# Which engine makes the low halves and the sums on SBUF tiles: chosen by stage

## The chip, the cores and the metric

One core of one Trainium2 chip runs the kernel. The metric is the device time of one execution in microseconds (us), the median of a few runs. Besides, one execution was recorded by the hardware profiler. Its rows use these names: PE is TensorE (matmuls), PEld its weight loads, DVE VectorE, ACT ScalarE, POOL GpSimd, SP SyncE, which issues nearly all DMAs here.

## The reference

One decoder layer in float32 with 2048 tokens, a width of 1024 and a hidden width of 2816:

```python
h = rmsnorm(x, g_mix[i])
z = h @ w_in[i]
zb, zc, zx, zq, zk, zv = jnp.split(z, ..., axis=-1)
y_c = zb * causal_dwconv3(zc * zx, conv_w[i], conv_b[i])
y_a = dilated_attention(rmsnorm(q), rmsnorm(k), v)
y = jnp.concatenate([rmsnorm(y_c, g_out_conv[i]), rmsnorm(y_a, g_out_attn[i])], axis=-1)
x = x + y @ w_out[i]                                        # the projection
h = rmsnorm(x, g_ffn[i])
gate = causal_dwconv3(h @ w_gate[i], ffn_conv_w[i], ffn_conv_b[i])
x = x + (jax.nn.silu(gate) * (h @ w_up[i])) @ w_down[i]     # gate and up, then the down-projection
ple_gate = jax.nn.sigmoid(rmsnorm(x, g_ple[i]) @ w_ple_gate[i])
x = x + ple_gate * (p[i].astype(x.dtype) @ w_ple_proj[i])
```

## The kernel before

Every float32 product is made of three fast matmuls. An operand x is split into a high half (`hi`, a cast by ACT, line 93) and a low half (`lo = x - hi`, a subtraction of two SBUF tiles, line 94), and `mm3` (line 97) adds hi·hi, hi·lo and lo·hi in PSUM. So each weight tile costs PE its matmuls, ACT one cast, and DVE or POOL one subtraction of 128x512 elements.

The program has three parts. `qkv` makes queries, keys and values. `mix` runs the attention and, in the gaps of it, the first convolution branch (`conv`): the product `zps`, the three taps (`ext`, `tap`, lines 248 to 257), the result `yc` (line 327), which also frees one of two PSUM banks. `rest`, which the change touches, is a list of stages that run one after the other:

- `project`, three times: y @ w_out in PSUM tiles of 128 tokens x 512. `split_y` (lines 824, 825) makes the operands `t` and `g` from y; `square` (lines 828, 830) sums the squares of y into `u`; `reciprocal_root` and `rsqrt` (lines 75 to 84, 838, 840: `ssy`, `rs_h` to `rsy`) make the factor by which line 902 scales a finished bank, adds x and so frees the bank.
- `prepare`, between them: `right` builds the seven right-hand operands of a Strassen-like product (seven instead of eight block products) from four blocks: four sums t1 to t4 (line 722), seven splits (`put`).
- `gate_up` for each half of the tokens: 11 blocks of hidden columns, each with seven products for the gate and seven for up. `left` makes the seven left operands (sums on line 702, splits on 94). In the first half `sums_of_w_down` also forms four differences of blocks of w_down (line 959, tile `g`) and stores them in DRAM (`td`), and `for_later` normalizes the other half's tokens.
- `down` for each half: seven products over 11 blocks, whose weights `raw` come from `td` or w_down; `finished` adds the parts (lines 1048, 1051).
- `ple`: the last two products.

Weights come from `stream`: it loads the next `raw` ahead of its use and has three split operands `w` made ahead of the one in use. The order of each engine's queue is not written by hand: a scheduler with a model of its own places the instructions, and each engine then works through its queue in that order, waiting on semaphores. `shared()` (line 87) gives DVE or POOL in turn for work that both can do: the splits of `stream` and `left`, the sums of `square`, the first sum in `finished`.

Of the kernel before, what the change touches and what calls it, by code (L numbers as in the profile page):

```python
# [16 lines left out]
ALU = mybir.AluOpType  # L17
# [22 lines left out]
class Layer:  # L40


    def __init__(self, tc, a, out, ctx):
        self.tc, self.nc, self.a, self.out, self.ctx = tc, tc.nc, a, out, ctx
        nc = self.nc
        self.turn = 0
        self.const = ctx.enter_context(tc.tile_pool(reuse_waits="tile", name="const", bufs=1))
        self.dram = ctx.enter_context(tc.tile_pool(name="dram", bufs=1, space=DRAM))
        self.ident = self.const.tile([P, P], F32, name="ident")
        make_identity(nc, self.ident)  # L50
        d = self.dram
        self.hd = [d.tile([KD, P, QT], F32, name=f"hd{c}") for c in range(NQ)]
        self.qd = [d.tile([2, 2, HD, SEQ], F32, name=f"qd{p}") for p in range(4)]
        self.kd = [d.tile([2, 2, HD, SEQ], F32, name=f"kd{p}") for p in range(4)]
        self.vd = [d.tile([QT, NH, 2 * HD], F32, name=f"vd{c}") for c in range(NQ)]
        self.ycd = [d.tile([P, SEQ], F32, name=f"ycd{i}") for i in range(4)]
        self.yad = [d.tile([P, SEQ], F32, name=f"yad{i}") for i in range(4)]
        self.xd = [[[d.tile([P, D], F32, name=f"xd{i}{c}{j}") for j in range(4)] for c in range(NQ)] for i in range(3)]
        self.gd = [d.tile([7, NF // 2, P, QT], F32, name=f"gd{h}") for h in range(2)]
        self.bd = [[d.tile([P, D], F32, name=f"bd{i}{j}") for j in range(4)] for i in range(2)]  # L60
        self.td = [d.tile([NF // 2, P, 2, 512], F32, name=f"td{i}") for i in range(2)]
        self.xq, self.pq, self.oq = [t.rearrange("(c j r) m -> c j r m", c=NQ, r=P) for t in (a["x"], a["p"], out)]
# [23 lines left out]

    def shared(self):

        self.turn = (self.turn + 1) % 3
        return self.nc.vector if self.turn else self.nc.gpsimd  # L90

    def split(self, hi, lo, src, lo_engine):
# [558 lines left out]
    def rest(self):  # L651
        nc, tc, a = self.nc, self.tc, self.a
        stages = [("project", (0, 1), (0,)), ("project", (0, 1), (1,)), ("prepare", 0), ("project", (2, 3), (0, 1)),
                  ("gate_up", 0), ("prepare", 1), ("down", 0), ("gate_up", 1), ("prepare_ple",), ("down", 1), ("ple",)]
        with ExitStack() as st:
# [59 lines left out]
            def right(at, b11, b12, b21, b22, temps, lo_engine):  # L715

                def put(i, x, engine):
                    hi, lo = at(i)
                    self.split(hi, lo, x, engine)

                t1, t2, t3, t4 = temps
                minus = lambda t, x, y: nc.vector.tensor_tensor(t, x, y, ALU.subtract)
                put(0, b11, lo_engine)
                yield
                minus(t1, b12, b11)
                put(4, t1, nc.vector)
                yield
                minus(t3, b22, b12)
                put(2, b22, lo_engine)
                yield  # L730
                minus(t2, b22, t1)
                put(6, t3, nc.vector)
                yield
                put(1, b21, lo_engine)
                yield
                minus(t4, b21, t2)
                put(5, t2, nc.gpsimd)
                yield
                put(3, t4, nc.gpsimd)
                yield  # L740

            def products(ops, quad, done):
# [169 lines left out]
            def prepare(h):  # L912
                self.quad = [new_quad(i > 3) for i in range(7)]
                if h:
                    for j in range(4):
                        b = [row("u") for _ in range(4)]
                        for x, (i, g) in zip(b, ((0, 0), (1, 0), (0, 1), (1, 1))):
                            nc.sync.dma_start(x, self.bd[i][j][:, 512 * g:512 * g + 512])
                        b = [x.rearrange("p (k n) -> p k n", n=P) for x in b]
                        yield from right(halves(self.quad, slice(j * P, j * P + P)), *b, [b[0], b[3], b[1], b[2]], nc.vector)  # L920
                    return
                self.g_ffn = gain("g_ffn")
                r = roots(0, 0, 8)
                for j in range(4):
                    xs = [load_tile(self.xd[1][i][j]) for i in range(2)]
                    for i, x in enumerate(xs):
                        normalize(x, r[:, 4 * i + j:4 * i + j + 1], self.g_ffn)
                    yield
                    b1 = []
                    for x in xs:  # L930
                        t = row("u").rearrange("p (k n) -> p k n", n=P)
                        nc.scalar.copy(t, transposed(x, 0))
                        b1.append(t)
                    b22, b21 = transposed(xs[1], 1), transposed(xs[0], 1)
                    for _ in right(halves(self.quad, slice(j * P, j * P + P)), *b1, b21, b22,
                                   [x[:, i:i + 512].rearrange("p (k n) -> p k n", n=P) for x in xs for i in (0, 512)], nc.vector):
                        pass
                    yield
# [14 lines left out]
            def sums_of_w_down(f):  # L953

                b = [operand("g").bitcast(F32) for _ in range(2)]
                for i, t in enumerate(b):
                    n = (2 * f + i) * P
                    nc.sync.dma_start(t.rearrange("p s n -> p (s n)"), a["w_down"][n:n + P])
                minus = lambda t, x, y: nc.vector.tensor_tensor(t, x, y, ALU.subtract)
                (b11, b12), (b21, b22) = [[t[:, s] for s in range(2)] for t in b]  # L960
                minus(b11, b12, b11)
                minus(b12, b22, b12)
                minus(b22, b22, b11)
                minus(b21, b21, b22)
                for d, t in zip(self.td, b):
                    nc.sync.dma_start(d[f], t)

            def gate_up(h):
                if h == 0:
                    background[0] = for_later()  # L970
                for f in range(NF // 2):
# [40 lines left out]
                    if h == 0:  # L1012
                        sums_of_w_down(f)
# [58 lines left out]
            def prepare_ple():  # L1072
                self.g_ple = gain("g_ple")
                self.quad = [new_quad(i > 3) for i in range(7)]
                for k in range(4):
                    b = [row("u") for _ in range(4)]
                    for x, (i, n) in zip(b, ((0, 0), (0, 1), (1, 0), (1, 1))):
                        nc.sync.dma_start(x, a["w_ple_gate"][(k + 4 * i) * P:(k + 4 * i + 1) * P, 512 * n:512 * n + 512])
                    yield from right(lambda i: (self.quad[i][:, k, 0], self.quad[i][:, k, 1]), *b,
                                     [b[0], b[3], b[1], b[2]], nc.vector)  # L1080
# [71 lines left out]
            ws = self.stream(raw_pool, operand, left, 3, stages)  # L1152
            run = dict(project=project, prepare=prepare, gate_up=gate_up, down=down, prepare_ple=prepare_ple, ple=ple)
            for name, *arg in stages:
                if name not in ("project", "down"):
                    for _ in background[0]:
                        pass
                if name.startswith("prepare"):
                    background[0] = run[name](*arg)
                    continue  # L1160
                run[name](*arg)
# [57 lines left out]
```

## Time and profile before

| what | value |
|---|---|
| median of 3 runs | 2756.98 us (2752.61 to 2761.0) |
| the profiled execution | 2758.95 us |
| its span from the first to the last instruction | 2757.2 us |
| PE busy | 2621.5 us, 95% of the span |
| DVE busy | 2006.8 us, 73% |
| ACT busy | 1321.2 us, 48% |
| POOL busy | 784.3 us, 28% |
| mean granted TensorE clock | 0.983 |

The profiled execution is 2.0 us above the median, and 1.75 us of it lie outside its span. The granted clock is the share of full speed (2.4 GHz) that TensorE was given; a fall shows as its lower level, half of that.

### The profile page before, as it was taken

Reading aid. Unit: us, or ns where it says so; the run is one execution under the profiler, and the core shown is the slowest. Engines: PE = TensorE matmul, PEld = TensorE weight load, DVE = VectorE, ACT = ScalarE, POOL = GpSimd, SP = SyncE. Lnnn points to the kernel's source line nnn. Section 1 sums busy time; section 2 is a strip of 40 time slices with the busy share of each in tenths; the row PEclk is TensorE's granted clock in tenths of the full one; section 3 lists DMA queues with packets and bytes.
Section 4 is the critical chain, followed back from the end, with each engine's and each line's share of the span. In section 5 each row is a group of like instructions: output and inputs, shape, how many; then the busy total and the mean of one; then the engine's idle time right before and its main releaser. Section 6 shows DMA issues by size and latency. Waiting matters only on the chain. (4 is left out here: it accounts for less than half of the span.)

```text
span 2757.2 us, 37506 instructions
## 1 busy us (share of the span) xinstructions
PE 2621.5 (95%) x12320; PEld 2169.0 (79%) x12320; DVE 2006.8 (73%) x3878; ACT 1321.2 (48%) x2941; POOL 784.3 (28%) x527
## 2 busy tenths in 40 slices
PE   7999989999999989899999999989999999998999
PEld 5777878888888778777788888767888887877887
DVE  8766656867677665998888778567888877557655
ACT  3332357877777344454344345444444435444332
POOL 5111311524343621123222223122222223223332
PEclk9999989999999999999999999999999999999999
DMA  5544565665756688568633346663323336666332
GB/s 191 153 138 123 169 163 139 184 184 146 205 154 180 220 279 296 196 228 274 241 114 105 107 142 227 216 233 115 102 101 107 104 111 218 220 217 204 103 130 85
DMA packets 283860, 470.04 MB, mean 170 GB/s; under 512 B 32656, under 2 KB 101904, under 8 KB 283664
## 3 DMA queue, kind: packets, MB, share of 16 engines
q1 hardware_dynamic: 283664, 467.64, 53.4%
q8 instruction: 97, 1.59, 0.2%
q14 instruction: 99, 0.81, 0.1%
HBM read 339.53 MB, written 127.99 MB: 170 GB/s over the span
## 5 line engine op out<-in xcount | busy, mean ns | idle before, releaser
L97 PE MATMUL ps<-t,w 128*128 128x512 f32 x4368 | 1024.3, 395 | 16.1 <-DVE w L94 9.5
L97 PEld LDWEIGHTS ps<-t,w 128*128 128x128 f32 x4368 | 819.6, 188 | 207.7 <-DVE w L94 12.4
L97 PE MATMUL ps<-w,g 128*128 128x512 f32 x1368 | 339.0, 397 | 26.9 <-DVE t L902 6.2
L97 PEld LDWEIGHTS ps<-w,g 128*128 128x128 f32 x1368 | 257.3, 190 | 89.0 <-DVE t L902 7.3
L94 POOL TENSOR_TENSOR w<-raw,w 128x512 fp32r<-128x512 f32 x100 | 144.9, 1449 | 564.1 <-ACT w L93 364.0
L97 PE MATMUL zps<-hq,chi 128*128 128x512 f32 x768 | 256.8, 411 | 5.3 <-DVE yc L327 5.3
L93 ACT CAST w<-raw 128x512 fp32r<-128x512 f32 x318 | 193.7, 616 | 119.5 <-PE ps L97 111.7
L289 POOL TENSOR_TENSOR clo<-craw,chi 128x512 fp32r<-128x512 f32 x96 | 126.4, 1322 | 389.8 <-ACT chi L288 144.2
L93 ACT CAST w<-s 128x512 fp32r<-128x512 f32 x208 | 128.3, 619 | 224.7 <-PE ps L97 200.5
L97 PE MATMUL ps<-w,t 128*128 128x512 f32 x852 | 211.6, 394 | 9.1 <-DVE w L94 5.9
L94 POOL TENSOR_TENSOR w<-s,w 128x512 fp32r<-128x512 f32 x70 | 111.8, 1597 | 368.7 <-ACT w L93 300.0
L438 ACT ACTIVATE pt<-so,md 128x256 f32<-128x256 f32 (+1 forms) x384 | 175.1, 458 | 79.9 <-DVE md L435 78.0
L97 PEld LDWEIGHTS ps<-w,t 128*128 128x128 f32 x852 | 159.0, 188 | 49.5 <-DVE w L94 8.8
L94 DVE TENSOR_TENSOR w<-raw,w 128x512 fp32r<-128x512 f32 x218 | 177.1, 816 | 15.5 <-ACT w L93 15.5
L435 DVE CUSTOM_DVE_ANT_0 so<-s,neg 128x256 f32<-128x256 f32 (+1 forms) x384 | 130.4, 362 | 60.9 <-PE s L432 47.3
L97 PEld LDWEIGHTS zps<-hq,chi 128*128 128x128 f32 x768 | 142.3, 195 | 29.6 <-DVE yc L327 6.1
L97 PE MATMUL zps<-hq,clo 128*128 128x512 f32 x384 | 154.3, 402 | 0.0
L432 PE MATMUL s<-kk,qs 128*128 128x256 f32 (+1 forms) x384 | 136.8, 360 | 11.8 <-DMA kk<-kd 9.1
L431 PE MATMUL s<-kk,qs 128*128 128x256 f32 (+1 forms) x384 | 132.8, 352 | 14.7 <-DMA kk<-kd 12.2
L471 DVE TENSOR_TENSOR nb<-po,nb 64x512 f32<-64x512 f32 x96 | 92.2, 961 | 65.0 <-ACT nb L470 64.2
L94 DVE TENSOR_TENSOR g<-g 128x512 fp32r<-128x512 f32 x84 | 72.6, 867 | 88.5 <-ACT g L93 88.5
L453 DVE TENSOR_TENSOR plo<-ptp,phi 128x512 fp32r<-128x512 f32 (+1 forms) x160 | 103.6, 653 | 30.9 <-ACT phi L452 30.2
(221 smaller groups left out, 4917.4 us busy)
## 6 DMA issues: line engine op xcount, KB each, us to landing
gd<-t SPq DMA_DIRECT2D x110, 256.0 KB, 2.0
craw<-in_w_conv_dram SPq DMA_DIRECT2D x96, 256.0 KB, 4.0
raw<-in_w_gate_dram SPq DMA_DIRECT2D x44, 512.0 KB, 3.8
raw<-in_w_up_dram SPq DMA_DIRECT2D x44, 512.0 KB, 3.7
g<-gd SPq DMA_DIRECT2D x84, 256.0 KB, 5.1
raw<-td SPq DMA_DIRECT2D x40, 512.0 KB, 4.5
t<-gd SPq DMA_DIRECT2D x70, 256.0 KB, 4.6
v<-vd SPq DMA_DIRECT2D x264, 64.0 KB, 2.7
```

Of the source, the lines that this page charges most:

```text
L93: self.nc.scalar.copy(hi, src)
L94: lo_engine.tensor_tensor(lo, src, hi.bitcast(F32), ALU.subtract)
L97: mm = lambda *a, **k: self.nc.tensor.matmul(*a, **k, **kw)
L289: nc.gpsimd.tensor_tensor(lo, raw, hi.bitcast(F32), ALU.subtract)
L431: mm(s[:, lo:], qb[l], cols[0], start=True, stop=False)
L432: mm(s[:, lo:], qb[l], cols[1], start=False, stop=True)
L435: nc.vector.tensor_tensor_reduce(out=so[:, lo:], in0=s[:, lo:], in1=neg[:, br, lo:], scale=-slope, scalar=3.0e38, op0=ALU.add, op1=ALU.min ...
L438: nc.scalar.activation(pt[:, l, lo:], so[:, lo:], AF.Exp, bias=md[:, 0, col:col + 1], scale=-1.0, accum_out=md[:, 1, col:col + 1])
L453: nc.vector.tensor_tensor(lo[:, i:i + n], tp[:, :n], hi[:, i:i + n].bitcast(F32), ALU.subtract)
L471: nc.vector.tensor_tensor(dst, like(po[other], br), dst, ALU.add)
```

## The change

Turns are counted in a cycle that the stage sets: 1 in `project`, so that every `shared()` is POOL; 2 in `down`; 3 elsewhere, as it was everywhere. In `right` the splits of t1 to t4 no longer have an engine of their own (two DVE, two POOL) but take turns, too. In `sums_of_w_down` two of the four differences go to POOL. The stage also decides for the generators that run in its background, as `prepare` does within `project` and `down`.

```diff
     def shared(self):
 
-        self.turn = (self.turn + 1) % 3
+        self.turn = (self.turn + 1) % self.cycle
         return self.nc.vector if self.turn else self.nc.gpsimd
...
                 minus(t1, b12, b11)
-                put(4, t1, nc.vector)
+                put(4, t1, self.shared())
...
-                put(6, t3, nc.vector)
+                put(6, t3, self.shared())
...
-                put(5, t2, nc.gpsimd)
+                put(5, t2, self.shared())
                 yield
-                put(3, t4, nc.gpsimd)
+                put(3, t4, self.shared())
...
-                minus = lambda t, x, y: nc.vector.tensor_tensor(t, x, y, ALU.subtract)
+                minus = lambda t, x, y: (nc.vector if t is b21 or t is b22 else nc.gpsimd).tensor_tensor(t, x, y, ALU.subtract)
...
             for name, *arg in stages:
+                self.cycle = dict(project=1, down=2).get(name, 3)
```

In the built programs 99 instructions of 128x512 elements change from DVE to POOL. Up to the end of the projection they are 23 splits of `w`, 16 sums of squares and 8 splits in `right` (which has 16 on POOL there, and had 8); of the 22 differences of w_down that move (22 stay), 7 stand in POOL's queue ahead of the first sums of `gate_up` on line 1007 and 15 behind; each `down` has 12 or 13 more splits on POOL. The sums of `finished` stay at 12 and 12. The scheduler places the rest of the queues anew. In the rows below the lines after the change are one higher than before (two from line 1156 on).

DVE's queue at the end of the convolution branch, from the reciprocal of the attention's denominators (`mx`) to the result `yc`. Before:

```order
L515 RECIPROCAL mx<-mx 32x128
L94 TENSOR_TENSOR w<-raw,w 128x512
L516 TENSOR_TENSOR e<-e,mx 32x384
L256 SCALAR_TENSOR_TENSOR tap<-ext,cw,tap 128x512
L94 TENSOR_TENSOR w<-raw,w 128x512
L257 SCALAR_TENSOR_TENSOR tap<-ext,cw,tap 128x512
L94 TENSOR_TENSOR w<-raw,w 128x512
L288 CAST chi<-craw 128x512
L94 TENSOR_TENSOR w<-raw,w 128x512
L327 TENSOR_TENSOR yc<-zps,tap 128x512
```

The same place after the change:

```order
L516 RECIPROCAL mx<-mx 32x128
L322 TENSOR_TENSOR ext<-zps,zc 128x512
L253 COPY ext<-carry 128x2
L517 TENSOR_TENSOR e<-e,mx 32x384
L249 COPY ext<-ext 128x2x31
L255 COPY carry<-ext 128x2
L257 SCALAR_TENSOR_TENSOR tap<-ext,cw,tap 128x512
L258 SCALAR_TENSOR_TENSOR tap<-ext,cw,tap 128x512
L289 CAST chi<-craw 128x512
L328 TENSOR_TENSOR yc<-zps,tap 128x512
```

The four splits of `w` have left the queue, and the reciprocal stands ahead of `ext` instead of behind it.

DVE's queue in the projection, from the copy of a sum of squares (`ssy`) into the chain of small instructions that makes the factor `rsy`. Before (the chain goes on with eight more small instructions, and two more of line 825 among them):

```order
L838 COPY ssy<-ps 128x4
L94 TENSOR_TENSOR w<-raw,w 128x512
L825 SCALAR_TENSOR_TENSOR g<-s,go,g 128x512
L75 TENSOR_SCALAR rs_h<-ssy 128x4
L94 TENSOR_TENSOR w<-raw,w 128x512
L76 TENSOR_SCALAR rs_i<-rs_h 128x4
L825 SCALAR_TENSOR_TENSOR g<-s,go,g 128x512
L77 TENSOR_SCALAR rs_y<-rs_i 128x4
L825 SCALAR_TENSOR_TENSOR t<-e,go,t 128x512
L82 TENSOR_TENSOR rs_u<-rs_y 128x4
L825 SCALAR_TENSOR_TENSOR t<-e,go,t 128x512
L83 TENSOR_TENSOR rs_u<-rs_u,rs_h 128x4
```

After (the chain goes on with five more small instructions, and none of line 826 among them):

```order
L839 COPY ssy<-ps 128x4
L76 TENSOR_SCALAR rs_h<-ssy 128x4
L77 TENSOR_SCALAR rs_i<-rs_h 128x4
L826 SCALAR_TENSOR_TENSOR g<-s,go,g 128x512
L78 TENSOR_SCALAR rs_y<-rs_i 128x4
L83 TENSOR_TENSOR rs_u<-rs_y 128x4
L84 TENSOR_TENSOR rs_u<-rs_u,rs_h 128x4
L85 SCALAR_TENSOR_TENSOR rs_y<-rs_u,rs_y 128x4
L83 TENSOR_TENSOR rs_u<-rs_y 128x4
L826 SCALAR_TENSOR_TENSOR g<-s,go,g 128x512
L84 TENSOR_TENSOR rs_u<-rs_u,rs_h 128x4
L826 SCALAR_TENSOR_TENSOR t<-e,go,t 128x512
```

Within the chain stood eight instructions of 128x512, and three are left.

POOL's queue in the projection, from the first sums of squares of the attention's half. Before:

```order
L830 TENSOR_TENSOR u<-u,e 128x512
L94 TENSOR_TENSOR w<-raw,w 128x512 x2
L830 TENSOR_TENSOR u<-u,e 128x512 x2
L94 TENSOR_TENSOR w<-raw,w 128x512
L830 TENSOR_TENSOR u<-u,e 128x512 x2
L94 TENSOR_TENSOR w<-raw,w 128x512
```

After:

```order
L831 TENSOR_TENSOR u<-u,e 128x512 x2
L95 TENSOR_TENSOR w<-raw,w 128x512
L831 TENSOR_TENSOR u<-u,e 128x512
L95 TENSOR_TENSOR w<-raw,w 128x512 x3
L831 TENSOR_TENSOR u<-u,e 128x512 x6
L95 TENSOR_TENSOR w<-raw,w 128x512 x3
```

Splits of weights now stand behind a run of six sums of squares.

## Rows read from the trace of the kernel before

**Rows 1.** The page: busy time of each engine, its share of the span, instructions.

```profile
PE 2621.5 (95%) x12320; PEld 2169.0 (79%) x12320; DVE 2006.8 (73%) x3878; ACT 1321.2 (48%) x2941; POOL 784.3 (28%) x527
```

**Rows 2.** Windows: stretch, length, busy (instructions) of PE, PEld, DVE, ACT, POOL; PEclk, DMA, GB/s.

```profile
900.00:985.00 85.00, 76.46 (x337) 62.12 (x334) 51.35 (x70) 26.47 (x45) 45.12 (x33) 0.96 0.67 214
985.00:1195.00 210.00, 196.59 (x892) 159.34 (x892) 162.13 (x321) 103.59 (x201) 35.19 (x25) 0.98 0.75 257
1195.00:1350.00 155.00, 141.10 (x620) 112.38 (x619) 139.27 (x206) 64.95 (x139) 40.05 (x23) 0.98 0.81 273
...
1640.00:1840.00 200.00, 190.74 (x819) 153.74 (x818) 131.90 (x174) 96.50 (x180) 51.80 (x34) 0.98 0.67 223
...
2280.00:2500.00 220.00, 207.95 (x889) 166.89 (x888) 146.04 (x197) 108.58 (x206) 57.42 (x36) 0.98 0.66 223
```

**Rows 3.** Lines, PE, of the last four stretches: busy, mean ns, idle before, who ended it.

```profile
L97 PE MATMUL ps<-w,g 128*128 128x512 f32 x552 | 135.4, 401 | 10.7 <-DVE t L902 6.2 <-DVE g L825 3.3 <-ACT g L824 1.1
...
L97 PE MATMUL ps<-t,w 128*128 128x512 f32 x556 | 136.1, 402 | 13.3 <-DVE w L94 9.0 <-POOL w L94 2.2 <-DVE u L753 1.9
...
L97 PE MATMUL ps<-w,g 128*128 128x512 f32 x326 | 82.2, 396 | 6.2 <-ACT g L93 2.4 <-DVE g L94 1.8 <-DVE w L94 1.7
L97 PE MATMUL ps<-w,t 128*128 128x512 f32 x271 | 68.3, 392 | 3.0 <-DVE w L94 2.3 <-POOL w L94 0.6
...
L97 PE MATMUL ps<-w,g 128*128 128x512 f32 x336 | 84.3, 395 | 6.9 <-DVE g L94 3.4 <-DVE w L94 1.7 <-ACT g L93 1.3
L97 PE MATMUL ps<-w,t 128*128 128x512 f32 x279 | 70.9, 394 | 5.2 <-DVE w L94 3.6 <-POOL w L94 1.1 <-ACT w L93 0.4
```

**Rows 4.** Timeline, 920:928, DVE, POOL, PE: start, us, engine, line [idle before <- releaser].

```profile
920.20 0.61 DVE L94 TENSOR_TENSOR w<-raw,w 128x512 fp32r<-128x512 f32 x1
...
921.87 1.77 DVE L94 TENSOR_TENSOR w<-raw,w 128x512 fp32r<-128x512 f32 x1
923.57 1.75 DVE L257 SCALAR_TENSOR_TENSOR tap<-ext,cw,tap 128x512 f32<-128x512 f32 x1
...
923.06 1.72 POOL L94 TENSOR_TENSOR w<-raw,w 128x512 fp32r<-128x512 f32 x1
...
927.50 0.79 PE L97 MATMUL zps<-hq,chi 128*128 128x512 f32 x1 [4.10 <-DVE yc L327]
```

**Rows 5.** Timeline, 1003:1015, DVE, then PE.

```profile
1003.37 0.15 DVE L838 COPY ssy<-ps 128x4 f32<-128x4 f32 x1
1003.44 0.68 DVE L94 TENSOR_TENSOR w<-raw,w 128x512 fp32r<-128x512 f32 x1
...
1008.09 1.24 DVE L83 TENSOR_TENSOR rs_u<-rs_u,rs_h 128x4 f32<-128x4 f32 x1
...
1012.94 0.17 DVE L840 COPY rsy<-rs_y 128x4 f32<-128x4 f32 x1
1013.02 0.69 DVE L830 TENSOR_TENSOR u<-u,e 128x512 f32<-128x512 f32 x1
...
1014.42 0.96 PE L97 MATMUL ps<-w,g 128*128 128x512 f32 x3 [3.21 <-DVE t L902]
```

**Rows 6.** Lines, DVE, 1640:1840: busy, mean ns of one | idle before.

```profile
L94 DVE TENSOR_TENSOR w<-raw,w 128x512 fp32r<-128x512 f32 x46 | 39.0, 855 | 0.7 <-ACT w L93 0.7
L94 DVE TENSOR_TENSOR g<-g 128x512 fp32r<-128x512 f32 x34 | 31.6, 930 | 36.4 <-ACT g L93 36.4
...
L94 DVE TENSOR_TENSOR t<-u,t 128x512 fp32r<-128x512 f32 x20 | 17.7, 903 | 3.5 <-ACT t L93 3.5
...
L1051 DVE TENSOR_TENSOR s<-ps,s 128x512 f32<-128x512 f32 x8 | 5.2, 683 | 0.0
```

**Rows 7.** Lines, DVE, 1195:1350.

```profile
L959 DVE TENSOR_TENSOR g<-g 128x512 f32<-128x512 f32 x41 | 30.4, 743 | 10.3 <-DMA g<-in_w_down_dram 10.2
```

**Rows 8.** Lines, POOL, 985:1195.

```profile
L94 POOL TENSOR_TENSOR w<-raw,w 128x512 fp32r<-128x512 f32 x10 | 14.3, 1426 | 93.1 <-ACT w L93 56.1 <-issue 29.8 <-DVE t L902 7.2
```

**Rows 9.** Timeline, POOL, 985:1012.

```profile
999.30 1.68 POOL L830 TENSOR_TENSOR u<-u,e 128x512 f32<-128x512 f32 x1 [28.01 <-ACT e L828]
```

More of the change, by code (lines that the diff above doesn't have):

```diff
@@ L46, in __init__ @@
         self.turn = 0
+        self.cycle = 1
         self.const = ctx.enter_context(tc.tile_pool(reuse_waits="tile", name="const", bufs=1))
```

## The prediction

> **What bounds the kernel now.** The page first: PE is busy for 95% of the span, DVE for 73%, POOL for 28% [rows 1]. So the kernel is bound by TensorE, and a change of the two other engines can only win back time in which PE waits, or add to it. Next the windows by stage [rows 2]: subtract PE's busy time from each stretch's length. The end of the convolution branch (900 to 985) leaves 8.5 us, the projection (985 to 1195) 13.4, the head of the first gate_up (1195 to 1350) 13.9, the first down (1640 to 1840) 9.3, the second (2280 to 2500) 12.1. The rest of each gate_up has next to none, so these five stretches with 57 us are all that the change can win by shorter waits. Beside the waits the granted TensorE clock shows 0.96 in the first stretch and 0.98 in the others, where full speed is 1.00. That is 0.04 x 85 = 3.4 us and 0.02 x 210 = 4.2 us in the first two, 3.1, 4.0 and 4.4 us in the others: 19 us more, which I take to go only where a long wait goes.
>
> Then PE's own groups, to see who ended its waits [rows 3]. In the projection it is DVE's line 902, which frees a bank (6.2 of 10.7 us in the main group), and DVE's operand `g` (3.3); no weight split appears. In the head of gate_up it is DVE's split of `w` (9.0 of 13.3). In the two downs it is `w` on DVE (1.7 and 2.3, then 1.7 and 3.6), `g` from ACT or DVE, and `w` on POOL (0.6 and 1.1). The reader is to see that DVE's queue ends most waits in all five, though often with an operand that this change leaves where it is.
>
> **What one moved instruction costs.** On DVE a 128x512 subtraction takes 0.61 us when nothing disturbs it [rows 4]; POOL takes 1.43 us for the same in the projection [rows 8]. POOL has the time: 35 of 210 us are used there [rows 2], and 47 moved instructions by 1.43 make 67 us more. But they disturb DVE. While POOL splits `w` at 923.06, DVE's tap at 923.57 takes 1.75 us; a neighbour of the same shape at 921.87 takes 1.77 [rows 4]. Against 0.68 us for the undisturbed shape, one of 683 ns [rows 6], that is 1.07 us for each DVE instruction that is caught. How often is it? In the first down the groups that read two SBUF tiles have means of 855, 930 and 903 ns, the one that reads PSUM 683 [rows 6]: 46 x 0.172 + 34 x 0.247 + 20 x 0.220 = 20.7 us of stretching beside 34 POOL instructions [rows 2], 0.61 us each. So in a stretch as a whole a move gives DVE 0.61 us and takes 0.61 back. The bounds are 0 (POOL runs while DVE reads PSUM or rests) and 1.07 (always caught).
>
> The Trainium skill has the rule behind these rows: in "SBUF — State Buffer", section "SBUF: two separate sides", GpSimd and a DVE instruction with two SBUF inputs take one shared port pair by an exclusive lock, and the loser waits for the whole instruction; "Perfetto Trace Analysis", section "Optimizing Scalar/DVE Operations", concludes that offloading between the two might not help. The trace agrees on the lock (1.75 against 0.68 us). By that conclusion the sum below would be nothing at all, and it speaks against this change.
>
> **The change part by part.** What can be won is therefore not DVE's total but what stands ahead of a late instruction in its queue.
>
> *End of the convolution.* PE waits 4.10 us, until 927.50, for `yc` to free a bank [rows 4]. In the 12 us before it DVE's queue holds five instructions that leave, one sum of squares and four splits: four of about 0.61 us and the caught one at 921.87 with 1.77, together 4.2 us. `ext` now waits for the reciprocal, but the same instructions are done before `yc` either way. POOL's convolution splits will catch another instruction in place of the caught one, 1.07 us. So the wait shrinks by 3.1 us, to 1.0, and I let the fall of the clock go with it: 3.1 + 3.4 = 6.5 us. Bounds: nothing, if two more are caught and `clo` on POOL comes late behind five splits of `w`; 7.5 us if none is caught.
>
> *Projection.* The example is PE's wait of 3.21 us before 1014.42 for line 902 [rows 5]. Its factor takes from `ssy` at 1003.37 to `rsy` at 1013.11, 9.7 us, because DVE does eight 128x512 instructions in between, and a sum of squares behind it. After the change three stand in between and none behind: six fewer, 6 x 0.61 = 3.7 us. Three of these moved to POOL, where they catch DVE at 0.61 us each: 1.8 us back, 1.9 us left. Two small instructions are caught there already, for 1.24 us as the one at 1008.09. With the wait shortened by more than half I count half of the stretch's clock loss, 2.1 us. In the other burst, at the first `prepare`, five leave and five more catch: nothing. Sum 4.0 us. Bounds: a loss of 5 us, if the moves there catch fully (47 x 0.46 = 22 us of DVE, of which a quarter falls into bursts), to 13.4 + 4.2 = 17.6 us won.
>
> *Head of gate_up.* 22 of the differences on line 959, 0.743 us each on DVE [rows 7], go to POOL. DVE is busy 139 of 155 us, and 10.3 of the rest it waits for the DMAs of these very tiles. At 0.61 given and 0.61 taken it is nothing. Bounds: 22 x 0.46 = 10 us lost; 9.0 us won, all waits for DVE's `w`.
>
> *Downs.* 12 of some 50 splits in each leave DVE: a quarter of the waits for its `w`, 9.3 / 4 = 2.3 us. POOL's share rises by half, and so do its 1.7 us: 0.8 us. Left 1.5 us won. DVE rests a third of the time there, and that hides what is caught; without that rest the price is 24 x 0.46 = 11 us.
>
> *Unchanged:* the splits of gate_up keep their cycle of three, the DMAs are as many as before, and the queues of the first 900 us keep their order on DVE.
>
> The sum: 6.5 + 4.0 + 0 + 1.5 = 12.0 us. Against the profiled execution's own 2758.95 this is 2747; that execution is 2.0 us above the median, so 2745 us against 2756.98, 0.43% faster. A difference under 0.3%, 8.3 us, can't be told from none with this kernel.
>
> **The rivals.** *Nothing is left of it.* What DVE gives up it loses again at the same places: in the bursts it is never idle, so each move catches fully there. For it: the average of 0.61 equals the price. Against it: in the examples the queue really is shorter. It would end anywhere from 2750 to 2764 us, about 2755. The rule of "Perfetto Trace Analysis" is this case.
>
> *Slower: POOL becomes the only source of weights in the projection.* Its queue now holds six sums of squares between splits of `w`, and a sum of squares waits for ACT, which waits for y from DRAM: POOL waited 28.01 us for one before 999.30 [rows 9]. Three operands are made ahead, each for 24 matmuls at 135.4 / 552 = 0.245 us, 17.7 us of cover. Six sums take 6 x 1.43 = 8.6 us, so it decides once the wait exceeds 9 us. Another 28.0 us would cost 28.0 + 8.6 - 17.7 = 18.9 us: 2757 + 19 = 2776 us. Against it: no wait of PE for POOL stands in the projection before, and the long wait there came when nothing else was due.
>
> *Much faster.* All waits and clock losses of the first two stretches' examples go (7.5 + 17.6 us), half of the head's 13.9 and a quarter of the downs' 21.4 too: 37 us, 2720 us. For it: waits feed one another. Against it: most enders in rows 3 stay on DVE.
>
> **How the numbers follow.** The forecast, 6 to 20 us faster, 0.36; much faster 0.12; nothing left 0.34; POOL's queue 0.10; fully caught bursts, some 10 us slower, 0.08. Of the forecast 0.02 falls under 8.3 us: faster 0.46, same 0.36, slower 0.18. The likeliest one's own range is 2737 to 2751. The range that leaves out 2 in 10 reaches from the much faster case, 2719, to 2772, short of the slow rival.
>
> **What would show it.** Right: no wait of 4 us for `yc` near 927, `rsy` within 6 us of `ssy`, a clock of 1.00 in the first stretch, DVE's busy time down by much less than 99 x 0.61 = 60 us, with more instructions of 1.2 us and over. Wrong: PE's waits in the projection ended by POOL's `w`; a longer sum of waits in the head of gate_up, ended by `w` or `g`; or the same waits merely handed to line 825.

## The result and the profile after

The change made the kernel slower: 2780.45 us (2779.21 to 2783.92, median of 4 runs) against 2758.99 us for the kernel before in the same session, a ratio of 1.0083 with a 95% interval of 1.0066 to 1.0100. The prediction was 2745 us, faster; its range ended at 2772.

First the page of the changed kernel, the line that answers to [rows 1].

```profile
PE 2628.1 (95%) x12320; PEld 2168.2 (78%) x12320; DVE 2010.7 (72%) x3779; ACT 1320.6 (48%) x2941; POOL 927.9 (33%) x626
```

DVE executes 99 instructions fewer and is busy 3.9 us longer; POOL gains 144 us. The 60 us that the moved instructions took on DVE came back as stretching of the others.

Where the time went is read from windows that begin and end with the same matmuls in both kernels, since the stages shift: the projection (it began at 975.64 and ended at 1189.43 before, 213.8 us), then the two downs. The window of the second down runs on into `ple`, up to its first transposition on line 1112 (1113 after the change), 7 to 11 us past the down's last matmul. Columns as in [rows 2]. The changed kernel:

```profile
978.01:1197.25 219.24, 201.28 (x898) 161.66 (x898) 164.02 (x287) 106.57 (x203) 92.31 (x64) 0.97 0.75 251
1647.47:1885.72 238.25, 224.40 (x950) 179.04 (x949) 146.90 (x185) 110.22 (x209) 81.67 (x54) 0.99 0.63 216
2309.44:2554.94 245.50, 226.30 (x967) 182.21 (x966) 163.21 (x201) 115.25 (x219) 86.53 (x55) 0.97 0.65 221
```

The two downs of the kernel before, measured so:

```profile
1637.32:1868.64 231.32, 221.20 (x950) 178.49 (x949) 148.46 (x197) 109.21 (x208) 59.92 (x40) 0.99 0.66 221
2291.62:2534.05 242.43, 225.67 (x968) 181.21 (x967) 157.82 (x213) 115.77 (x219) 68.70 (x42) 0.98 0.67 223
```

Of 22.2 us between the two profiled executions, the windows of the downs hold 6.9 + 3.1 = 10.0 and the projection 5.4; the rest is scattered. The downs alone hold 6.9 + 2.2 = 9.1, since the second takes 234.0 us before and 236.2 after. These are single profiles, and among the profiles of the 19 kernels below the projection begins anywhere from 972 to 984 us, so a few us in one stretch of one of them tell little. In the first down DVE is less busy than before and POOL rests two thirds of the time, so neither is the bound there. PE's waits in that down, changed kernel (engine and line that waited, engine and line that ended it: us in all, times, longest):

```profile
PE ps L98 <- POOL w L95: 5.6, 7, 1.2
PE ps L98 <- DVE t L95: 2.5, 1, 2.5
PE ps L98 <- DVE g L95: 1.9, 1, 1.9
PE ps L98 <- DVE w L95: 1.7, 3, 1.0
PE ps L98 <- ACT w L94: 1.4, 3, 0.6
PE ps L98 <- ACT g L94: 0.6, 1, 0.6
```

The same before:

```profile
PE ps L97 <- DVE w L94: 3.9, 4, 1.7
PE ps L97 <- ACT g L93: 2.4, 1, 2.4
PE ps L97 <- POOL w L94: 1.9, 3, 0.9
PE ps L97 <- DVE g L94: 1.8, 1, 1.8
```

Before, waits for POOL's `w` there came to 1.9 us in three pieces. Now they are seven of 0.8 us or so, and three end with ACT's copy of `w`: late before either low-half engine comes into it. The waits add up to 13.7 us against 10.0. The other 3.2 us of the 6.9 stand in PE's busy time (224.40 against 221.20 us for the same 950 matmuls), whose ends the profile models.

At the end of the convolution branch PE's longest wait of `zps` for `yc` fell from 4.10 to 2.7 us (compare [rows 4]) and the clock of that stretch rose from 0.96 to 0.99. But all its waits for `yc` came to 6.0 us in three pieces where they were 5.3 in two, and `ext` is waited for, too (the window, PE's waits in it, and the wait of the kernel before):

```profile
900.00:985.00 85.00, 72.81 (x318) 57.54 (x317) 48.93 (x62) 26.63 (x46) 58.69 (x43) 0.99 0.64 203
```

```profile
PE zps L98 <- DVE yc L328: 6.0, 3, 2.7
PE zps L98 <- DVE ext L322: 1.8, 2, 1.5
```

```profile
PE zps L97 <- DVE yc L327: 5.3, 2, 4.1
```

In the projection DVE's instruction that makes `g` (line 825 before, 776 ns a piece) is now the one that is caught, and PE waits 6.9 us for it where it waited 3.3 [rows 3], while its waits for line 902 (now 903) fell from 6.2 to 2.6. DVE and PE, changed kernel, that window:

```profile
L826 DVE SCALAR_TENSOR_TENSOR g<-s,go,g 128x512 fp32r<-128x512 f32 x48 | 48.5, 1021 | 22.1 <-ACT g L825 21.9
PE ps L98 <- DVE g L826: 6.9, 7, 1.9
PE ps L98 <- DVE t L903: 2.6, 2, 2.3
```

The kernel before:

```profile
L825 DVE SCALAR_TENSOR_TENSOR g<-s,go,g 128x512 fp32r<-128x512 f32 x47 | 35.8, 776 | 14.4 <-ACT g L824 14.3
PE ps L97 <- DVE g L825: 3.3, 4, 1.4
PE ps L97 <- DVE t L902: 6.2, 3, 3.2
```

### The profile page after: what moved, and what is told of

Its sections match the earlier page's. It is cut to its first block, busy times and chain, and to the rows that moved or that the text cites. A ratio compares the mean times of both kernels' runs of the same rounds, so it can differ in the third digit from the quotient of the medians.

```text
span 2779.3 us, 37541 instructions
## 1 busy us (share of the span) xinstructions
PE 2628.1 (95%) x12320; PEld 2168.2 (78%) x12320; DVE 2010.7 (72%) x3779; ACT 1320.6 (48%) x2941; POOL 927.9 (33%) x626
## 4 chain that ended last, share of the span: by engine, by line
PE 39%; DVE 9%; DMA 8%; issue 5%; POOL 2%; ACT 1%; SPq 0%; DVEq 0%; POOLq 0%; ACTq 0%
PE ps L98 38%; DMA g<-gd 2%; DVE t L95 1%; DVE w L95 1%; POOL w L95 1%; DMA t<-gd 1%; DMA g<-in_w_down_dram 1%; DMA u<-bd 1%; DMA bd<-g 1%; DVE g L95 1%; DVE g L826 1%; DVE u L723 1%; DMA u<-in_w_ple_gate_dram 1%; DMA td<-g 0%; DMA g<-xd 0%
## 5 line engine op out<-in xcount | busy, mean ns | idle before, releaser
L95 POOL TENSOR_TENSOR w<-raw,w 128x512 fp32r<-128x512 f32 x154 | 226.9, 1476 | 477.0 <-ACT w L94 384.7
L95 DVE TENSOR_TENSOR w<-raw,w 128x512 fp32r<-128x512 f32 x164 | 143.6, 877 | 3.9 <-ACT w L94 3.8
L454 DVE TENSOR_TENSOR plo<-ptp,phi 128x512 fp32r<-128x512 f32 (+1 forms) x160 | 103.7, 654 | 30.9 <-ACT phi L453 29.7
```

The lines of the kernel that those rows point to most:

```text
L95: lo_engine.tensor_tensor(lo, src, hi.bitcast(F32), ALU.subtract)
L454: nc.vector.tensor_tensor(lo[:, i:i + n], tp[:, :n], hi[:, i:i + n].bitcast(F32), ALU.subtract)
```

## Experiments

All were timed beside the kernel before, which stood at 2756.5, 2759.4, 2760.2, 2759.7 and 2758.7 us in the five sessions of the e, f, g, h and i kernels. The table gives medians, ratios, and the windows of the two downs in the profiled execution; in brackets stands the second down alone, from its first to its last matmul.

| kernel | us | ratio, 95% interval | downs, us |
|---|---|---|---|
| before | 2756.5 to 2760.2 | | 231.3, 242.4 (234.0) |
| changed | 2780.5 | 1.0083 [1.0066, 1.0100] | 238.2, 245.5 (236.2) |
| e1_project | 2752.8 | 0.9984 [0.9974, 0.9995] | 227.1, 238.7 (227.3) |
| e2_down | 2757.0 | 1.0000 [0.9987, 1.0013] | 232.2, 241.4 (230.7) |
| e3_sums | 2759.4 | 1.0006 [0.9994, 1.0018] | 229.3, 239.9 (231.7) |
| e4_right | 2753.6 | 0.9988 [0.9976, 1.0001] | 228.6, 234.3 (226.0) |
| f1_no_project | 2782.7 | 1.0090 [1.0071, 1.0110] | 235.6, 251.3 (240.9) |
| f2_no_down | 2759.0 | 1.0003 [0.9989, 1.0016] | 229.4, 234.1 (225.9) |
| f3_no_sums | 2781.9 | 1.0089 [1.0070, 1.0107] | 235.5, 249.6 (240.4) |
| f4_no_right | 2761.6 | 1.0015 [1.0003, 1.0027] | 228.5, 234.8 (226.2) |
| g1_pair | 2776.5 | 1.0056 [1.0044, 1.0068] | 236.1, 249.6 (239.3) |
| g2_turned | 2766.6 | 1.0026 [1.0012, 1.0041] | 230.4, 242.7 (232.1) |
| g3_own_turn | 2762.7 | 1.0015 [1.0000, 1.0029] | 230.7, 233.9 (225.9) |
| g4_turned_no_right | 2771.2 | 1.0034 [1.0022, 1.0046] | 230.0, 240.4 (230.6) |
| h1_queue | 2750.8 | 0.9970 [0.9957, 0.9984] | 221.7, 234.8 (227.7) |
| h2_phase_alone | 2752.3 | 0.9974 [0.9961, 0.9987] | 226.5, 236.4 (227.9) |
| h3_queue_before | 2742.3 | 0.9944 [0.9927, 0.9961] | 220.4, 234.6 (225.7) |
| i1_own_turn_queue | 2749.8 | 0.9963 [0.9950, 0.9975] | 224.4, 229.7 (221.2) |
| i2_phase_queue | 2738.5 | 0.9922 [0.9901, 0.9943] | 218.5, 230.6 (221.8) |

**One part at a time, on the kernel before.** Each takes one of the change's hunks:

```diff
# e1_project
+                self.cycle = dict(project=1).get(name, 3)
# e2_down
+                self.cycle = dict(down=2).get(name, 3)
# e3_sums: the hunk of sums_of_w_down. e4_right: the four hunks of right
```

> Only the cycle of 1 in the projection; right, the differences of w_down and the cycle of 3 elsewhere as before. Against the kernel before, the changed kernel lost about 5 us up to the end of the projection, 3 in the head of gate_up, 7 in the first down and 4 in the second. Lock theory (in bursts DVE and POOL take turns at SBUF, so a moved instruction lengthens the burst): 4 to 6 us slower, all of it between 980 and 1200, nothing in the downs. Theory of late weights (a split is simply later on POOL, 1.4 instead of 0.6 us, and PE waits for it): the same total, but PE's waits in the projection are ended by w on POOL. Theory of the order (the scheduler's new queues decide, whatever was moved): any time within 8 us either way, and the losses of the four parts don't add up to 19.

> Only the cycle of 2 in down. Lock theory: 9 to 13 us slower, in the two downs alone, and DVE's instructions there are stretched by 6 to 14 us more in each. Theory of late weights: as much slower, with PE's waits for w on POOL up from 1.7 to over 8 us in the two downs together. Theory of the order: within 8 us either way, no tie to the downs.

> Only two of the four differences of w_down on POOL. Lock theory: 2 to 4 us slower between 1190 and 1380, where DVE is never idle. Theory of late weights: no change, for no weight split moves. Theory of the order: within 8 us either way.

> Only the turns in right, at the cycle of 3: of 16 splits in each prepare about 5 on POOL instead of 8. Lock theory: no change to 2 us faster, as a few fewer instructions stand on POOL. Theory of late weights: no change. Theory of the order: within 8 us either way.

None is slower than the kernel before by what can be told, and e1 is a little faster; the medians' differences (-3.7, +0.5, +2.9, -2.9) add up to -3 us, where all parts together cost 22. No price of a single part explains the result: neither the sums, nor the projection's late weights, nor a price for each caught instruction. Yet a total can hide a price: e1's projection is some 5 us longer, as its first theory expected, while its downs, which its part leaves alone, are shorter. With the cycle of 1 the projection takes 217 to 220 us in nine of ten profiles (215 in i1), without it 211 to 215 in all nine.

**One part left out of the changed kernel.**

```diff
# f1_no_project
-                self.cycle = dict(project=1, down=2).get(name, 3)
+                self.cycle = dict(down=2).get(name, 3)
# f2_no_down
+                self.cycle = dict(project=1).get(name, 3)
# f3_no_sums: the hunk of sums_of_w_down undone. f4_no_right: the hunks of right undone
```

> The changed kernel with the cycle of 3 kept in the projection (2 in down, right and the differences of w_down as changed). The four parts by themselves gave -4, 0, +3 and -3 us, together the change gave +22, so the loss lies in combinations. Theory of pairs (right's turns fall badly where the cycle is 1 or 2): about 8 us come back, 2772, in the projection and the head of gate_up, and the downs keep their loss of 10. Theory of a threshold (POOL and DVE collide more than in proportion once enough work is on POOL): every part left out gives back 3 to 8 us. Theory of the order (each set of turns is another draw of the queues): anything from 2745 to 2785, in stretches that the part does not touch as well.

> The changed kernel with the cycle of 3 kept in down. Theory of pairs: the loss of 10 us in the two downs goes, 2770. Threshold: 3 to 8 us come back. Order: anything from 2745 to 2785.

> The changed kernel with all four differences of w_down on DVE. Theory of pairs: 0 to 4 us come back. Threshold: 3 to 8 us, in the projection's end and the head of gate_up. Order: anything from 2745 to 2785.

> The changed kernel with right's fixed engines (two splits of t on DVE, two on POOL). Theory of pairs: most of the loss goes, 2755 to 2762, in the projection and in both downs. Threshold: 3 to 8 us come back, in the projection alone, since right has as many splits on POOL in the downs as before. Order: anything from 2745 to 2785.

The loss stays in full without the projection's part and without the sums. It goes without `right`'s turns, and it goes without the cycle of 2. So it is a pair, and the theory of pairs missed which: f1 did not fall to 2772 and f2 fell below 2770. (f1's projection takes 211 us again, but its profile lost as much elsewhere, 4.7 us in the second down.) Yet f4 has as many POOL instructions in the downs as the changed kernel.

**The pair, and which instructions fall on which engine.** The generator `right` runs in the background of a down, a step after every third weight. Both take turns from one counter, so a turn of `right` shifts all weights behind it. g1 has the pair alone; g2 swaps the engines; g3 gives `right` a counter of its own; g4 is the swap without `right`'s turns.

```diff
# g1_pair: the kernel before, the four hunks of right, and
+                self.cycle = dict(down=2).get(name, 3)
# g2_turned (changed kernel), g4_turned_no_right (f4_no_right)
                 self.cycle = dict(project=1, down=2).get(name, 3)
+                if name == "down":
+                    self.turn = 0
# g3_own_turn: changed kernel, self.turn = 1 at the same place, put(..., self.own()) for t1 to t4, and
+    def own(self):
+        if self.cycle != 2:
+            return self.shared()
+        self.mine = not self.mine
+        return self.nc.vector if self.mine else self.nc.gpsimd
```

The turns of the third product of a down and the start of the fourth, as the program counts them (weight by product and place, P is POOL, d is DVE, in brackets a split of `right`; in the second row `right` counts by itself and is left out):

```
changed   2.0d 2.1P 2.2d 2.3P 2.4d [P] 2.5d 2.6P 2.7d 2.8P 2.9d 2.10P [d] 3.0P 3.1d 3.2P 3.3d 3.4P [d] 3.5P
own turn  2.0d 2.1P 2.2d 2.3P 2.4d     2.5P 2.6d 2.7P 2.8d 2.9P 2.10d     3.0P 3.1d 3.2P 3.3d 3.4P     3.5d
```

> The kernel before with only the two parts whose absence removed the loss: right takes turns, and the cycle is 2 in the down-projections. If the pair is the whole of it: 2772 to 2785, both downs together some 10 us longer than before. If the projection or the sums are needed too: 2755 to 2765. If no pair loses and the loss lies in something that the parts left out shift by chance: about 2757.

> The changed kernel with the turn set at the start of each down-projection so that every instruction that GpSimd takes there goes to VectorE and the other way round: as many on each engine, other ones. If which instructions fall on GpSimd decides (their phase): 2755 to 2768, since the starting phase that loses is left. If it is the number on GpSimd, or that weights and right's low halves take turns from one counter at all: 2775 to 2785 as in the changed kernel.

> The changed kernel, but in the down-projections right's four low halves alternate by a counter of their own, so that the weights alternate without a break; as many instructions on GpSimd as in the changed kernel within two. If right's turns lose by shifting the weights' alternation (three weights between two steps, then two turns of the same engine close together): 2757 to 2765. If they lose by the low halves that GpSimd now has of the first two differences, or by the number: 2775 to 2785.

> The changed kernel with right's fixed engines (2761.6) and the alternation in the down-projections started on the other engine, as it stands in the kernel with the cycle of 2 alone. If the starting phase decides there: 2768 to 2775 (in single profiles the two downs of that phase were 10 us longer). If it does not: 2758 to 2764.

g1 shows the pair by itself, with 16 of the 22 us. In the four profiles that have the pair as it stands in the changed kernel (changed, f1, f3, g1) the two downs alone take 474 to 477 us, in all others with the loads where they were 454 to 466. g3 removes 18 us of the loss with the same work on each engine. Its downs, to be held against the windows above:

```profile
1648.90:1879.56 230.66, 221.55 (x950) 180.35 (x949) 149.05 (x185) 109.82 (x210) 80.28 (x54) 0.98 0.66 222
2304.80:2538.72 233.92, 223.13 (x967) 182.37 (x966) 159.23 (x201) 116.48 (x219) 85.24 (x55) 0.98 0.69 232
```

The counts are 185 and 201 on DVE, 54 and 55 on POOL in both kernels, the busy times agree within 4 us, and the two windows are 19 us shorter together. g2 leaves 6 of 22 us, and g4 is 10.9 us above the kernel before where f4 is 2.2 above, by no other edit than the phase of an unbroken alternation. So the number on POOL does not decide; which instructions fall there does.

**Why a low half that is late by a microsecond stays late.** This is a timeline of the changed kernel in the second down (start, us, engine, line, operation; in brackets the idle time and who ended it; SPq is SyncE issuing DMAs; rows of PE's weight loads and others left out):

```profile
2465.84 1.30 POOL L95 TENSOR_TENSOR w<-raw,w 128x512 fp32r<-128x512 f32 x1 [9.93 <-ACT w L94]
...
2467.17 0.37 SPq L620 DMA_DIRECT2D raw<-td  x1
...
2467.41 1.43 POOL L95 TENSOR_TENSOR w<-raw,w 128x512 fp32r<-128x512 f32 x1 [0.27 <-ACT w L94]
2467.61 1.78 DVE L95 TENSOR_TENSOR w<-raw,w 128x512 fp32r<-128x512 f32 x1
2467.63 0.42 SPq L1036 DMA_DIRECT2D t<-gd  x1
2469.42 0.37 SPq L620 DMA_DIRECT2D raw<-td  x1
...
2469.88 0.42 SPq L1036 DMA_DIRECT2D g<-gd  x1
...
2475.33 0.62 ACT L94 CAST g<-g 128x512 fp32r<-128x512 f32 x1 [2.87 <-DMA g<-gd]
2475.86 0.61 ACT L94 CAST w<-raw 128x512 fp32r<-128x512 f32 x1
...
2476.52 0.50 PE L98 MATMUL ps<-w,t 128*128 128x512 f32 x1 [0.89 <-ACT w L94]
2476.59 0.68 DVE L95 TENSOR_TENSOR w<-raw,w 128x512 fp32r<-128x512 f32 x1
...
2477.33 0.95 PE L98 MATMUL ps<-w,t 128*128 128x512 f32 x3 [0.31 <-DVE w L95]
```

Read it from the bottom. PE waited 0.89 us for ACT's copy of a weight. That copy stood in ACT's queue behind the split of a product `g`, for whose load from DRAM ACT had idled 2.87 us. The load was issued at 2469.88, right behind a load of raw weights in SyncE's queue, and that one was issued at 2469.42, when DVE's low half from 2467.61 had ended at 2469.39: the low half was the last reader of the raw tile that the load overwrites. It had taken 1.78 us beside POOL's split of 2467.41; undisturbed it takes 0.68, as at 2476.59. So it is a ring: low half, raw load, product load, ACT's queue, weight, low half. A delay anywhere can go round it, and the product load takes 5.4 us of this round.

Followed back in the same way, six of the 16 waits of the changed kernel's first down, from 1815 to 1868, run through a product load that was issued right behind such a raw load, less than 10 us earlier: 3.4 of 13.7 us. Before it is two of nine (1.8 of 10.0 us), in g3 none of five. So the ring was there before, and it holds 1.6 of the 3.7 us by which the waits of that down grew; it is part of the loss and not shown to be all of it. Other waits there follow runs of low halves on POOL or bursts of DVE. SyncE stood this long before raw loads in that down, changed kernel (us in all, times, longest):

```profile
SPq L620 <- DVE w L95: 78.8, 24, 8.5
SPq L620 <- POOL w L95: 26.8, 12, 7.5
```

h1 and h3 cut the ring. The product loads leave SyncE's queue, and nothing else is edited (the scheduler places the queues anew):

```diff
-                        nc.sync.dma_start(g, self.gd[h][m, f])
+                        nc.scalar.dma_start(g, self.gd[h][m, f])
```

h2 tests the price of the phase without the change's other parts: e2 with `self.turn = 1` at the start of each down.

> The changed kernel with the loads of the kept products (g and t from gd, in the down-projections) issued by ScalarE instead of SyncE, so that they no longer stand in SyncE's queue behind the load of raw weights, which waits for the last low half of an earlier raw tile. If the broken alternation loses through that ring (low half late, raw load late, product load late, ScalarE's queue held by the product's copy with the weight's copy behind it): the downs fall back to 460 to 472 us together and the time to 2755 to 2768. If the low halves themselves come too late whatever the loads do: 2775 to 2785.

> The kernel before with the cycle of 2 in the down-projections alone, as in the run that made no difference (2757.0), but with the first weight of each down-projection on GpSimd instead of on VectorE. If the phase of an unbroken alternation is worth what the two kernels without right's turns showed (2761.6 against 2771.2, the downs 462 against 469 us): 2745 to 2752, faster than the kernel before. If that difference came from something else: 2755 to 2760.

> The kernel before with the product loads of the down-projections issued by ScalarE, as a control for the same edit in the changed kernel. If the ring through SyncE's queue costs the kernel before its waits in the down-projections too (473 us against 462 in the best kernels): 2743 to 2752. If the edit only costs ScalarE time: 2757 to 2770.

All three are faster than the kernel before. h1 is below both of its ranges (its windows of the downs are 456.6 us together), h3 is just below its own, and h2 just above its first. The changed kernel gains 30 us by the edit of one word; its 238.2 us of first down become 221.7. PE's waits there are all of this:

```profile
PE ps L98 <- DVE t L95: 2.6, 1, 2.6
PE ps L98 <- DVE w L95: 0.7, 1, 0.7
PE ps L98 <- POOL w L95: 0.5, 2, 0.3
```

Its timeline in the second down shows the two loads (ACTq) issued while SyncE is held back between two raw loads, 3.7 and 3.3 us ahead of the second:

```profile
2443.38 0.36 SPq L620 DMA_DIRECT2D raw<-td  x1
...
2445.01 0.33 ACTq L1036 DMA_DIRECT2D g<-gd  x1
2445.37 0.44 ACTq L1036 DMA_DIRECT2D t<-gd  x1
...
2448.69 0.32 SPq L620 DMA_DIRECT2D raw<-td  x1
```

SyncE still stands before raw loads in h1's first down, 90.3 + 30.9 = 121 us against 106 in the changed kernel; what is gone is the product loads behind them. Not separated is a second effect of the same edit: the loads run on a DMA queue of their own (q10 in h1's profile, 10234 packets in that down) and land sooner, by about 1 us (rows of the last section), and no run tells how much of the gain is that.

The kernel before gains 17 us by it (h3), so waits of its own in the downs hung on the same queue. h2 is faster by 0.26% where e2, with the other phase, made no difference.

**One mechanism or two.** i1 joins g3 and h1, i2 joins h2 and h3.

> The changed kernel with both cures: right's own counter in the down-projections (2762.7 by itself) and the product loads issued by ScalarE (2750.8 by itself). If the broken alternation loses only through the load queue, nothing is left for the counter to give: 2747 to 2755. If the two cures remove different losses: 2730 to 2740.

> The kernel before with the unbroken cycle of 2 in the down-projections in its better phase (2752.3 by itself) and the product loads issued by ScalarE (2742.3 by itself). If the phase, too, is paid through the load queue: 2738 to 2745, as with the loads alone. If the two add: 2732 to 2737.

With the loads out of SyncE's queue the counter gives nothing more (2749.8 against 2750.8): what the broken alternation costs, it costs only while they stand in that queue. i2 is the fastest of all, 0.78% under the kernel before and 42 us under the changed one, but its interval overlaps that of h3, so what the phase still gives there can't be told.

## Why the prediction was wrong

**The step that failed is *Downs*.** It took a quarter off the waits for DVE's `w`, added half to POOL's, and came to 1.5 us won; measured are 9.1 us lost in the downs alone (10.0 in the windows). It read who ended PE's waits and stopped there: `w` on DVE was taken for a long DVE queue. But DVE rested a third of the time, which the step itself says, so its queue was not what made `w` late. The row on ACT's idle time and the queue behind the loads were not asked: taking the product loads out of SyncE's queue brought the two windows from 483.7 to 456.6 us (h1), with the splits on the same engines. The price that the step held ready, 11 us if the cover is gone, has the right size, but its mechanism, more caught instructions, is not what happened: g3 has as many on each engine and loses nothing like it. (Its 12 splits are too few, too: by the program's turns POOL has 23 of a down's 77 splits of `w` before and 38 after, some of them executed ahead of the down's first matmul.)

***Unchanged* hid the cause.** "The DMAs are as many as before" is true, and their count is not their time. The coupling by the shared counter was not seen either: the prediction prices a cycle of 2 and `right`'s turns as two numbers of moved instructions, and their joint order costs more than both.

**One moved instruction** was sized well: 0.61 given and 0.61 taken was forecast, and 99 moves gave back all of their 60 us and 3.9 more, 0.65 each. (The forecast's average left out five smaller groups of the same window that read two SBUF tiles; with them it is 24.6 us, 0.72 each.) That sum, over a whole stage, did not tell what PE waits for.

**Projection:** 4.0 us won was forecast, 5.4 lost; the lower bound of this term (a loss of 5) was right, by its own reason, that the moves catch the instructions of the bursts. What the sum counted on did come, for PE waits 3.6 us less for line 902; what it called a sign of being wrong came, too, for the waits were handed to line 825, 3.6 us more. The chain from `ssy` to `rsy`, 9.7 us in [rows 5], still takes 8.5 us (1005.66 to 1014.19), because those left in it are stretched: line 826 at 1008.08 takes 1.86 us, a small one at 1006.95 takes 1.21. In e1 the same part costs some 5 us in the projection, and e1 is no slower because its downs, which its turns enter in another phase, are shorter (4.2 us, and 6.7 in the second down alone); that the phase is the reason is not shown.

**End of the convolution:** the wait of 4.10 us shrank to 2.7 and the fall of the clock went as forecast, but the stretch became 0.8 us longer instead of 6.5 shorter, with more waits for `yc` and `ext`. **Head of gate_up:** forecast 0, measured 1.0 us longer, which one pair of profiles can't tell from none; within it the waits for DVE's `w` fell from 9.0 to 3.2 us, and those for POOL's `w` (2.2 to 4.8) and for DVE's `u` (1.9 to 4.6) took their place.

**The rivals.** "POOL becomes the only source of weights in the projection" gave 2776 us, close to the measured time, for a reason that did not occur: no wait of PE for POOL stands in that stage, and f1, without that part, is as slow. The number was right by accident, and it counts a sum at 1.43 us, the time of a split, where [rows 9] has 1.68.

**What stays open:** why the changed kernel's phase loses 22 us and the swapped one of g2 only 6. The scheduler places the queues anew for each kernel, and its share was not separated from that of the engines. How the gain of h1 divides between the ring, other waits on the queue and loads that land sooner is open, too. Between h1 and h3 8.5 us are left; their profiles put 6.5 us into the projection, where h1 has the cycle of 1 and h3 has not.

## What to carry to other kernels

When an engine that is not busy is named as the end of TensorE's waits, follow the late instruction back through its queue, to the load in it and to what that load stood behind; here moving one kind of load out of one queue gave 17 us to the kernel before and 30 to the changed one. A counter from which several places draw turns couples all stages behind it, so single parts don't add up (here -3 against +22 us): give each place its own counter, or set the phase, before pricing one. Loads that could go at once should not stand in one queue behind loads that wait for a buffer.

## What the runs showed of the hardware

Issuing the 71 product loads of the first down from ScalarE left its own work as it was: it is busy 109.9 us there against 110.2 in the changed kernel. That figure doesn't count issues. They took 25.2 us of its queue (0.33 us in the median, 1.4 at most), and all but 0.7 us of that ran while an instruction of ScalarE was executing, as at 2445.01 in h1, beside a cast from 2444.90 to 2445.52. The loads landed sooner, in a median of 3.9 us for `g`, where the profile tells both ends. The windows are h1's two downs, and its DMA rows for the first follow (out<-in, queue, operation, count, KB each, median us from issue to landing):

```profile
1639.78:1861.51 221.73, 217.90 (x950) 178.73 (x949) 148.50 (x185) 109.89 (x209) 80.04 (x54) 0.99 0.70 232
2285.50:2520.34 234.84, 222.58 (x967) 181.44 (x966) 157.42 (x201) 115.20 (x219) 85.36 (x55) 0.99 0.70 231
```

```profile
g<-gd ACTq DMA_DIRECT2D x38, 256.0 KB, 3.9
t<-gd ACTq DMA_DIRECT2D x33, 256.0 KB, 4.0
```

In the changed kernel the same loads, on SyncE's queue, took 4.6 and 5.3 us:

```profile
g<-gd SPq DMA_DIRECT2D x38, 256.0 KB, 4.6
t<-gd SPq DMA_DIRECT2D x33, 256.0 KB, 5.3
```

Not expected in this form was that DVE and POOL, both reading SBUF, take turns where both queues are full. DVE's rows and then POOL's, changed kernel, start of the first down:

```profile
1668.54 3.48 DVE L95 TENSOR_TENSOR t<-u,t 128x512 fp32r<-128x512 f32 x2
1671.95 1.76 DVE L723 TENSOR_TENSOR u<-u 128x512 f32<-128x512 f32 x1
```

```profile
1668.04 1.74 POOL L1008 TENSOR_TENSOR t<-t,c 128x512 f32<-128x512 f32 x1
1669.73 1.75 POOL L95 TENSOR_TENSOR t<-u,t 128x512 fp32r<-128x512 f32 x1
1671.43 1.72 POOL L95 TENSOR_TENSOR w<-raw,w 128x512 fp32r<-128x512 f32 x1
```

Each of DVE's takes some 1.75 us and ends half a microsecond after one of POOL's, and each of POOL's takes as long: a pair needs 1.7 us, where DVE alone needs 0.68 and POOL some 1.3. The Trainium skill, "SBUF — State Buffer", section "SBUF: two separate sides", names an exclusive lock on a port pair that the two share. The trace agrees that the loser waits; the pair's 1.7 us is 0.2 to 0.3 less than the sum of the two alone, so they still seem to overlap a little.
